# Final SSD states with the state dimension as stationary operand, in rounded products, three of four groups behind the mixer norm's sums

## The chip, the cores and the metric

The kernel runs on one core of a Trainium2 chip. The metric is the device time of one execution in microseconds (us). The engines that matter here are TensorE (PE, matrix products; its weight loads are listed as PEld), VectorE (DVE), ScalarE (ACT), GpSimd (POOL, which also issues DMAs) and SyncE (SP, which issues most of the DMAs).

## The reference

One layer of a streaming encoder, for a prompt of 256 new frames and for a sample of 32 next frames of a running stream, with the same weights. All of it is computed in full precision:

```python
proj = rmsnorm(x) @ w_in                       # u_pool | z | x, B, C | dt
y_pool = pool_mixer(u_pool)                    # trailing means, windows 2, 4, 8, 16
y_ssd, new_ssd = ssd_mixer(z, xBC, dt, state)  # Mamba-2 scan, gated, normed
mix = concat([y_pool, y_ssd]) @ w_out          # 3072 -> 2048
x = x + rmsnorm(mix, norm_mix_post)
up = conv3(rmsnorm(x, norm_ffn_pre) @ w_up)    # 2048 -> 11264
x = x + rmsnorm((silu(gate) * val) @ w_down, norm_ffn_post)   # 5632 -> 2048
```

The change is about one output of the mixer, the final state of the scan. For each of 32 heads (64 channels each; 16 heads share one B of 128 values)

```python
state[head, channel, n] = decay * state_before[head, channel, n] \
    + sum over tokens of  w[token, head] * x[token, head, channel] * B[token, n]
```

where `w` is the time step times the decay from the token to the end. The prompt starts with a state of zero; the sample has a state before. So the prompt's state is a product over 256 tokens and the sample's one over 32 tokens plus a scaled history, each 2048 channels by 128 values. Outputs are `y` for both streams, these states, and the last rows of the convolutions and the pooling.

## The kernel before, in words

**Products.** Activations stand transposed, channels on the 128 partitions and the 288 tokens (256 of the prompt, then 32 of the sample) in the columns. Each full-precision product of the projections is made of three products of rounded operands (`fp32r`): the activation is split into a rounded part and the rest, the weight into `whi` and `wlo`, and `mm3` (L141 to L144) adds high by high, high by low and low by high in one accumulator. A weight tile comes by a DMA that SP issues (`fetch_w`, L117, 1 MB into `raw`), ACT rounds it (`whi`, L136) and DVE subtracts (`wlo`, L137). `project` runs over the K pieces of a projection and, for each piece, over the column groups (256 columns, two accumulators each). `raw`, `whi` and `wlo` have a few buffers each, so that loads run some tiles ahead.

**Order.** The instructions of each engine are put in order by a planner that simulates the queues; `tc.high_priority` moves an instruction ahead of its place in the program, `pin` and `tc.keep_in_program_order` hold it to it. Tiles of one `tag` share its `bufs` buffers; who asks for a tile waits until an older one of the tag is done with.

**The w_out stage.** Its activations are `mixp` (eight pooling tiles) and `mixs` (sixteen SSD tiles). Seven calls of `project` cover column groups (0, 1), 2, 3, 4, 5, 6, 7; the K pieces of each are tiles 8 to 15, 16 to 23 and 0 to 7. When an accumulator is done, `mix_out` squares it on ACT, POOL adds the square to `msum` (`sq_add`, L677), and ACT writes the scaled copy `mg` to SBUF. The sum over the 2048 channels, which are spread over partitions, is a product with a matrix of ones in full precision: `msum` of the first fourteen tiles goes in at the start of group 7 (L956), and the squares of the last two follow by themselves (L852). Then come the root (L976, ACT), the reciprocal (L977, DVE), for each of sixteen tiles a multiplication and the addition of the residual (L988, L989, DVE), and the rounded and the low part of `hn` (L993 on ACT, L994 on DVE), which the w_up products read. `xsum` (L1002, L1006) collects squares for the next norm.

**The states.** Earlier, the scan has written the convolved x and B by token to DRAM (`xs_d`, `b_d`), and the weights `w` to `tokd`. The states are products in full precision (not split; the profile counts two PE instructions for each):

- `states_of(g)`, g = 0, 1, each four tiles of 128 channels, after w_out groups 2 and 4. POOL issues seven loads (x of the prompt, x of the sample, state before), DVE multiplies by `w` and the decay, and PE makes, for each tile, two products over 128 prompt tokens (L905) and one over the 32 sample tokens on 32 partitions (L911). The stationary operand is x by token, the moving one B: channels come out on partitions, n in 128 columns. ACT copies, DVE adds the history, SP stores.
- `state_in(t)` and `state_mm(t)`, t = 8 to 15, one tile of 128 channels each: three loads on POOL (L926), two multiplications on DVE, three products (L938; for the sample the last 128 tokens, with B set to zero where they are the prompt's). `state_mm(8)` stands between the last two sums of the norm, the other seven behind them, ahead of the first `hn` product on PE. ACT copies (L942), POOL adds the history (L943), SP stores two tiles (L944, L945).
- `pwq` is a set of four small products that spread the sample's `w` over four sets of 32 partitions, at the start of the w_out stage.

The buffers `du` (four, of the size of two 288-column tiles) hold pooling tiles at the start of the stage and the operands of the states after it.

## Time and profile before

| | |
|---|---|
| median of three runs | 1336.0 us (1335.72 to 1336.15) |
| span of the profiled execution (first to last instruction) | 1333.3 us |
| time around that span, by the median | 2.7 us |
| PE busy | 1325.7 us, 99% |
| DVE, ACT, POOL busy | 885.5 us (66%), 665.1 us (50%), 241.7 us (18%) |
| w_out stage | about 303 to 475 us |
| norm, from the last w_out product to the first `hn` product | 475.1 to 481.5 us |
| w_up (with w_down in turns from 762 us), then the end of w_down | 481.5 to 1324.9 us |
| granted PE clock | 1.000 |

The page gives the profiled execution its span alone, without a time of its own beside it. In the rows of the timeline the columns are the start in us, the length in us, the engine, the line of the kernel, the operation and the tiles it writes and reads, with "xN" for N instructions drawn together; in brackets stands how long the engine had been idle before, and what ended that. In the rows of groups, the numbers behind the bar are the busy time in us, the mean of one in ns, and, after the second bar, the idle time before them. PE's instructions overlap in its pipeline: the time that one takes from the stream is the distance of starts, not the length of a row. A row with two or more products runs from the first start to the last end.

### The profile page before, as it was taken

What the parts mean: (1) busy time and instruction counts of PE and PEld (TensorE: products, weight loads), DVE (VectorE), ACT (ScalarE), POOL (GpSimd) and SP (SyncE); (2) the same over time, 40 slices, a digit from 0 to 9 for tenths busy, and PEclk for the clock granted to TensorE, in tenths of its full rate; (3) what the DMA queues carried; (4) which work ended last, traced back from release to release, by engine and by line L of the source; (5) the groups of instructions that cost most, each with busy time, mean ns of one, the idle gap of its engine ahead of it and who ended that gap; (6) DMA issues with size and microseconds to landing.
All of it is one profiled execution on the core that took longest, in us unless ns stands there. A gap on an engine that the chain in (4) does not pass through costs nothing.

```text
span 1333.3 us, 25388 instructions
## 1 busy us (share of the span) xinstructions
PE 1325.7 (99%) x10127; PEld 1314.2 (99%) x10127; DVE 885.5 (66%) x1501; ACT 665.1 (50%) x995; POOL 241.7 (18%) x386
## 2 busy tenths in 40 slices
PE   9999999999999999999999999999999999999998
PEld 9999999999999999999999999999999999999997
DVE  7999987879544488976766643335666666754454
ACT  7557767446443456544444433334454444444442
POOL 2343231222122310211211200001121111201110
PEclk9999999999999999999999999999999999999999
DMA  8678884455555446766554454454554555466753
GB/s 329 192 216 266 272 252 156 155 199 210 190 191 202 143 145 227 210 184 181 167 177 158 153 172 156 160 182 162 179 165 159 167 170 170 159 227 188 206 177 111
DMA packets 110230, 249.52 MB, mean 187 GB/s; under 512 B 64480, under 2 KB 75840, under 8 KB 87584
## 3 DMA queue, kind: packets, MB, share of 16 engines
q1 hardware_dynamic: 105920, 233.61, 54.6%
q0 software_dynamic: 3808, 13.77, 2.9%
q8 instruction: 79, 1.29, 0.4%
q10 hardware_dynamic: 384, 0.52, 0.1%
q14 instruction: 39, 0.32, 0.1%
HBM read 235.91 MB, written 11.95 MB: 186 GB/s over the span
## 4 chain that ended last, share of the span: by engine, by line
PE 98%; DVE 0%; DMA 0%; ACT 0%; SPq 0%; issue 0%
PE acc L142 30%; PE acc L144 30%; PE acc L143 30%; PE acc L355 2%; PE acc_x L355 1%; PE py L613 1%; PE acc L1200 0%; PE acc L1201 0%; DMA xg<-in_x_g 0%; PE acc_t L1223 0%; PE pst L938 0%; PE acc_x L143 0%; PE acc_x L142 0%; PE acc_x L144 0%; PE pst L905 0%; PE py L615 0%
## 5 line engine op out<-in xcount | busy, mean ns | idle before, releaser
L137 DVE TENSOR_TENSOR wlo<-raw,whi 128x1024 fp32r<-128x1024 f32 (+1 forms) x396 | 472.0, 1193 | 346.1 <-ACT whi L136 344.8
L136 ACT ACTIVATE whi<-raw 128x1024 fp32r<-128x1024 f32 (+1 forms) x396 | 408.5, 1033 | 503.2 <-PE acc L143 420.4
L142 PE MATMUL acc<-hn,whi 128*128 128x288 f32 x1376 | 404.3, 296 | 0.0
L143 PE MATMUL acc<-hn,whi 128*128 128x288 f32 x1376 | 403.8, 294 | 0.2 <-DVE hn L994 0.2
L144 PE MATMUL acc<-hn,wlo 128*128 128x288 f32 x1376 | 403.3, 294 | 0.0
L143 PEld LDWEIGHTS acc<-hn,whi 128*128 128x128 f32 x1376 | 259.9, 189 | 0.7 <-DVE hn L994 0.7
L144 PEld LDWEIGHTS acc<-hn,wlo 128*128 128x128 f32 x1376 | 259.9, 189 | 0.0
L142 PEld LDWEIGHTS acc<-hn,whi 128*128 128x128 f32 x1376 | 257.3, 187 | 0.1
L142 PE MATMUL acc<-fa,whi 128*128 128x288 f32 x660 | 195.5, 296 | 0.0
L143 PE MATMUL acc<-fa,whi 128*128 128x288 f32 x660 | 195.4, 296 | 0.0
L144 PE MATMUL acc<-fa,wlo 128*128 128x288 f32 x660 | 195.1, 296 | 0.0
L142 PE MATMUL acc<-xn,whi 128*128 128x288 f32 x608 | 180.8, 297 | 0.0
L143 PE MATMUL acc<-xn,whi 128*128 128x288 f32 x608 | 179.1, 295 | 0.0
L144 PE MATMUL acc<-xn,wlo 128*128 128x288 f32 x608 | 178.8, 294 | 0.0
L143 PEld LDWEIGHTS acc<-fa,whi 128*128 128x128 f32 x660 | 124.5, 189 | 0.0
L142 PEld LDWEIGHTS acc<-fa,whi 128*128 128x128 f32 x660 | 124.1, 188 | 0.0
L144 PEld LDWEIGHTS acc<-fa,wlo 128*128 128x128 f32 x660 | 123.8, 188 | 0.0
L1027 POOL COPY fc_stage<-ebuf 128x4 f32<-128x4 f32 x88 | 25.7, 293 | 503.5 <-DVE ebuf L1026 460.1
L143 PEld LDWEIGHTS acc<-xn,whi 128*128 128x128 f32 x608 | 114.9, 189 | 0.1
L144 PEld LDWEIGHTS acc<-xn,wlo 128*128 128x128 f32 x608 | 114.8, 189 | 0.0
L142 PEld LDWEIGHTS acc<-xn,whi 128*128 128x128 f32 x608 | 114.0, 187 | 0.8 <-issue 0.5
L1033 DVE SCALAR_TENSOR_TENSOR fc<-ebuf,cols,fc 128x290 f32<-128x290 f32 x176 | 90.4, 517 | 2.9 <-ACT fc L1031 0.3
(333 smaller groups left out, 1766.5 us busy)
## 6 DMA issues: line engine op xcount, KB each, us to landing
raw<-in_w_up SPq DMA_DIRECT2D x80, 1024.0 KB, 5.1
raw<-in_w_in SPq DMA_DIRECT2D x38, 1024.0 KB, 5.4
raw<-in_w_down SPq DMA_DIRECT2D x32, 1024.0 KB, 5.0
raw<-in_w_out SPq DMA_DIRECT2D x24, 1024.0 KB, 5.0
raw<-in_w_down SPq DMA_DIRECT2D x16, 768.0 KB, 4.2
raw<-in_w_up SPq DMA_DIRECT2D x14, 512.0 KB, 3.9
gb<-g_d POOLq DMA_DIRECT2D x8, 832.0 KB, 7.1
raw<-in_w_first SPq DMA_DIRECT2D x5, 768.0 KB, 13.0
```

What stands on the lines that cost most here:

```text
L136: act.activation(hi, raw[:, k : k + n, :], AF.Copy)
L137: dve.tensor_tensor(lo, raw[:, k : k + n, :], hi.bitcast(F32), op=ALU.subtract)
L142: then(pe.matmul(out, wh, a[:, 0, :], start=start, stop=False))
L143: then(pe.matmul(out, wh, a[:, 1, :], start=False, stop=False))
L144: then(pe.matmul(out, wl, a[:, 0, :], start=False, stop=stop))
L355: pin(pe.matmul(first[m], w[:, k, r * NB + m * P :][:, :P], xn[kb + k][:, x, :], start=kb + k + r + x == 0, stop=kb + k == KD - 1 and r == ...
L613: ins = pe.matmul(y[c, 0:256], xw[:, 0, f_], m[:, h, 0:256], start=True, stop=False)
L1027: pool.tensor_copy(fc_stage[:, :, :, i], e[:, 256:324].rearrange("p (s c) -> p s c", c=34)[:, :, 0:2])
L1033: dve.scalar_tensor_tensor(c, e[:, r_ : r_ + 290], f_w[:, r_, i : i + 1], c, op0=ALU.mult, op1=ALU.add)
```

## The change

- **The other way round.** The stationary operand of a state product is now B by token (128 tokens by 128 values of n) and the moving one x times `w` with 512 channels: n comes out on partitions and 512 channels in the columns. Four groups g = 0 to 3 of 512 channels take the place of two `states_of` and eight `state_mm`. The state outputs are laid out (n, channel), and the host turns them.
- **Rounded products.** B is split once into `bt_h` and `bt_l`, x times `w` for each group into `xh` (ACT) and `xl` (DVE), and a prompt's group takes six products (two blocks of 128 tokens, each high by high, high by low, low by high).
- **96 partitions.** The sample's 32 tokens stand three times above each other, x as (high, low, high) and B as (high, high, low), so that one product over 96 partitions sums the three terms. `raw_s` and `xq` are loaded three times for it, and `pwq` makes `w` for 96 partitions; it moves to an earlier place, beside `phv`, which gets a second small product for the decays.
- **History.** `history` loads 256 channels of the state before at a time (POOL), multiplies by the decay (DVE) and writes the result to a DRAM tile `hd` (SP), after w_out groups 2 to 5. `state_out` copies a group's two accumulators (ACT), stores the prompt's (SP), adds `hd` to the sample's by a DMA that accumulates (POOL's queue), and stores that (SP).
- **Place.** Group 0 is made after w_out group 2. The operands of group 1 are prepared after group 4, those of groups 2 and 3 after group 5. The products of group 1 come behind the last w_out product, five of them ahead of the norm's sums and two behind; groups 2 and 3 follow behind the sums, and the copies of group 3 stand behind the second tile's `hn`.
- **The norm's sums.** Column groups 6 and 7 go through `project` together. The early sum at group 7 leaves. `msum` takes fifteen squares, the last square stays by itself, both are split into a rounded and a low part, and four rounded products with a rounded matrix of ones follow. `xsum` uses the buffer of `msum`.
- **Buffers.** `du` has six instead of four and takes the pooling tiles' `dpool` as well. The first group's outputs `ho` and the raw operands `xr` are in it; groups 2 and 3 keep their split operands in the buffers of the `hn` tiles (`atile`).

The diff, cut to its core (the removed functions are named above):

```diff
+    p_ = aux([P, HEADS], "pwq")
+    wq = const.tile([P, HEADS], F32, name="wq")
+    for j in range(3):
+        pe.matmul(p_[NS * j : NS * (j + 1), :], ident[:, P - NS :], tokd[:, 2, :], start=True, stop=True)
+    dve.tensor_copy(wq[: 3 * NS], p_[: 3 * NS])
+    hv = htile("hv", NX + HEADS)
     elast = htile("elast", 1)
     act.activation(elast, g[:, 415:416], AF.Exp)
     dve.tensor_scalar(hv[:, 0:NX], pick, hp[:, 2:3], None, op0=ALU.mult)
-    dve.tensor_scalar(hv[:, NX:], pick, elast, None, op0=ALU.mult)
-    p_ = aux([P, 2 * NX], "phv")
-    pe.matmul(p_, sel64.rearrange("h r q -> h (r q)"), hv, start=True, stop=True)
-    dcol = const.tile([P, 2 * NX], F32, name="dcol")
+    dve.tensor_scalar(hv[:, NX:], id32, elast, None, op0=ALU.mult)
+    p_ = aux([P, NX + HEADS], "phv")
+    pe.matmul(p_[:, :NX], sel64.rearrange("h r q -> h (r q)"), hv[:, :NX], start=True, stop=True)
+    pe.matmul(p_[:, NX:], ones[:HEADS, :], hv[:, NX:], start=True, stop=True)
+    dcol = const.tile([P, NX + HEADS], F32, name="dcol")
...
-        d = op_.tile([P, NT], F32, tag="dpool", bufs=2, name="dpool")
+        d = op_.tile([P, 2, NT], F32R, tag="du", bufs=6, name="dpool")[:, 0, :].bitcast(F32)
...
-        a = op_.tile([P, 2, NT], F32R, tag="du", bufs=4, name="du")
+        a = op_.tile([P, 2, NT], F32R, tag="du", bufs=6, name="du")
...
+    ones_r = op_.tile([P, P], F32R, name="ones_r")
+    act.activation(ones_r, ones, AF.Copy)
...
-    last_sq = []
     def mix_out(p_):
         m = len(x1)
         o = btile("mg")
         if m < KD - 2:
             sq_add(msum, p_, op_, m == 0)
+        elif m == KD - 2:
+            with tc.high_priority(offset=400):
+                q = op_.tile([P, NT], F32, tag="sq", bufs=2, name="sq")
+                act.activation(q, p_, AF.Square)
+                dve.tensor_tensor(msum, msum, q, op=ALU.add)
         else:
-            q = op_.tile([P, NT], F32, name=f"msq{m}")
             with tc.high_priority(offset=400):
-                act.activation(q, p_, AF.Square)
-            last_sq.append(q)
-        if m == KD - 1:
-            for i, q in enumerate(last_sq):
-                if i:
-                    state_mm(LATE, *late_in[0])
-                tc.keep_in_program_order(pe.matmul(p_m, ones, q, start=False, stop=i == 1))
+                lows_ = op_.tile([P, 2, NT], F32R, tag="du", bufs=6, name="mlo")
+                last_sq = op_.tile([P, 318], F32, tag="win", bufs=3, name="last_sq")[:, :NT]
+                parts = [lows_[:, 0, :], lows_[:, 1, :]]
+                for i, q in enumerate((msum, last_sq)):
+                    h_ = op_.tile([P, NT], F32R, tag="sq", bufs=2, name="mhi")
+                    if i:
+                        pin(act.activation(q, p_, AF.Square))
+                        pin(dve.tensor_copy(h_, q))
+                    else:
+                        pin(act.activation(h_, q, AF.Copy))
+                    pin(dve.tensor_tensor(parts[i], q, h_.bitcast(F32), op=ALU.subtract))
+                    parts.append(h_)
+            def sums():
+                for i, q in enumerate((2, 0, 3, 1)):
+                    pin(pe.matmul(p_m, ones_r, parts[q], start=i == 0, stop=i == 3))
+            state_mm(1, *state_ops[1], between=sums)
...
-    btok = op_.tile([P, 2, 3, P], F32, name="btok")
...
+    bt_h, bt_l = (op_.tile([P, 2, 2, P], F32R, name=n) for n in ("bt_h", "bt_l"))
+    bt_s = bpool.tile([P, NT], F32R, tag="b", name="bt_s")[:, : 2 * P].rearrange("p (g c) -> p g c", g=2)
+    raw_b = op_.tile([P, 2, NT], F32, tag="du", bufs=6, name="raw_b")
+    raw_b = raw_b.rearrange("p r c -> p (r c)")[:, : 4 * P].rearrange("p (g b c) -> p g b c", g=2, b=2)
+    raw_s = op_.tile([P, 318], F32, tag="win", bufs=3, name="raw_s")[: 3 * NS, : 2 * P]
     for gi in range(2):
         c = slice(gi * P, (gi + 1) * P)
-        sp.dma_start(out=btok[:, gi, 0:2, :], in_=b_d[:NP_, c].rearrange("(b p) c -> p b c", p=P))
-        if gi:
-            pool.memset(btok[: P - NS, gi, 2, :], 0.0)
-            sp.dma_start(out=btok[P - NS :, gi, 2, :], in_=b_d[NP_:, c])
+        sp.dma_start(out=raw_b[:, gi], in_=b_d[:NP_, c].rearrange("(b p) c -> p b c", p=P))
+    for j in range(3):
+        sp.dma_start(out=raw_s[NS * j : NS * (j + 1), :], in_=b_d[NP_:, :])
+    act.activation(bt_h, raw_b, AF.Copy)
+    dve.tensor_tensor(bt_l, raw_b, bt_h.bitcast(F32), op=ALU.subtract)
+    s_ = bt_s.rearrange("p g c -> p (g c)")
...
+    act.activation(s_[: 3 * NS], raw_s, AF.Copy)
+    rows_ = slice(2 * NS, 3 * NS)
+    dve.tensor_tensor(s_[rows_], raw_s[rows_], s_[rows_].bitcast(F32), op=ALU.subtract)
...
+    def unit(name, ahead_=False):
+        t = atile(name) if ahead_ else op_.tile([P, 2, NT], F32R, tag="du", bufs=6, name=name)
+        return t.rearrange("p r c -> p (r c)")[:, : 4 * P]
+    def state_in(g, ahead_=False):
+        xl = [unit("xl", ahead_) for _ in range(2)]
+        xh = [unit("xh", ahead_) for _ in range(2)]
+        s = unit("xs", ahead_)
+        for b in range(2):
+            raw = unit("xr").bitcast(F32)
+            for i in range(2):
+                pool.dma_start(
+                    out=raw[:, 2 * P * i : 2 * P * (i + 1)], in_=xs_d[2 * g + i][b * P : (b + 1) * P, :]
+                )
+            o = raw.rearrange("p (r q) -> p r q", r=8)
+            w = tokd[:, b, 8 * g : 8 * g + 8]
+            dve.tensor_tensor(o, o, w.unsqueeze(2).broadcast_to([P, 8, 64]), op=ALU.mult)
+            act.activation(xh[b], raw, AF.Copy)
+            dve.tensor_tensor(xl[b], raw, xh[b].bitcast(F32), op=ALU.subtract)
+        for i in range(2):
+            c = slice(2 * P * i, 2 * P * (i + 1))
+            t = op_.tile([P, 318], F32, tag="win", bufs=3, name="xq")[: 3 * NS, : 2 * P]
+            for j in range(3):
+                pool.dma_start(out=t[NS * j : NS * (j + 1), :], in_=xs_d[2 * g + i][NP_:, :])
+            o = t.rearrange("p (r q) -> p r q", r=4)
+            heads = slice(8 * g + 4 * i, 8 * g + 4 * i + 4)
+            dve.tensor_tensor(o, o, wq[: 3 * NS, heads].unsqueeze(2).broadcast_to([3 * NS, 4, 64]), op=ALU.mult)
+            act.activation(s[: 3 * NS, c], t, AF.Copy)
+            r_ = slice(NS, 2 * NS)
+            dve.tensor_tensor(s[r_, c], t[r_], s[r_, c].bitcast(F32), op=ALU.subtract)
+        return xh, xl, s
+    hd = dram.tile([P, D_SSD], F32, name="hd")
+    def history(g):
+        for i in range(2):
+            heads = slice(8 * g + 4 * i, 8 * g + 4 * i + 4)
+            c = slice(4 * P * g + 2 * P * i, 4 * P * g + 2 * P * (i + 1))
+            h = btile("h")[:, : 2 * P]
+            pool.dma_start(out=h, in_=state_nq[:, c])
+            o = h.rearrange("p (r q) -> p r q", r=4)
+            w = dcol[:, NX:][:, heads]
+            dve.tensor_tensor(o, o, w.unsqueeze(2).broadcast_to([P, 4, 64]), op=ALU.mult)
+            sp.dma_start(out=hd[:, c], in_=h)
...
+    def state_mm(g, xh, xl, s, between=None):
+        gi = g // 2
+        st = acc_ps.tile([P, 4 * P], F32, tag="acc", name="pst")
+        st_s = aux([P, 4 * P], "pst") if g < 3 else acc_ps.tile([P, 4 * P], F32, tag="acc", name="pst")
+        todo = [(bt_h, xh, 0), (bt_h, xl, 0), (bt_l, xh, 0), (bt_h, xh, 1), (bt_h, xl, 1), (bt_l, xh, 1)]
+        for i, (w_, x_, b) in enumerate(todo):
+            if between and i == 5:
+                between()
+            pin(pe.matmul(st, w_[:, gi, b, :], x_[b], start=i == 0, stop=i == 5))
+        pin(pe.matmul(st_s, bt_s[: 3 * NS, gi, :], s[: 3 * NS], start=True, stop=True))
+        if g == 3:
+            return [g, st, st_s]
+        state_out(g, st, st_s)
+    def state_out(g, st, st_s):
+        if g:
+            ho, ho_s = (op_.tile([P, 2 * NT], F32, tag=f"mixp{2 * g - 2 + i}", bufs=1, name="ho") for i in range(2))
         else:
+            ho, ho_s = (unit("ho").bitcast(F32) for _ in range(2))
+        ho, ho_s = ho[:, : 4 * P], ho_s[:, : 4 * P]
+        for o, s in ((ho, st), (ho_s, st_s)):
+            ins = act.activation(o, s, AF.Copy)
+            if g == 3:
+                pin(ins)
+        c = slice(4 * P * g, 4 * P * (g + 1))
+        sp.dma_start(out=new_ssd_p[:, c], in_=ho)
+        pool.dma_start(out=ho_s, in_=hd[:, c], accum_op=ALU.add)
+        sp.dma_start(out=new_ssd_s[:, c], in_=ho_s)
+    state_ops = {}
...
-            if g == 7 and kb == 0:
-                pe.matmul(p_m, ones, msum, start=True, stop=False)
...
-    for grp in ((0, 1), (2,), (3,), (4,), (5,), (6,), (7,)):
+    for grp in ((0, 1), (2,), (3,), (4,), (5,), (6, 7)):
...
-        if grp[0] in (2, 4):
-            states_of(grp[0] // 2 - 1)
-        elif grp[0] == 6:
-            late_in[:] = [state_in(t, t >= LATE + 4) for t in range(LATE, NX - 2)]
+        if 2 <= grp[0] < 6:
+            history(grp[0] - 2)
+        if grp[0] == 2:
+            state_mm(0, *state_in(0))
+        elif grp[0] == 4:
+            state_ops[1] = state_in(1)
+        elif grp[0] == 5:
+            state_ops[2] = state_in(2, True)
+            state_ops[3] = state_in(3, True)
...
-    late_in += [state_in(t, ahead_=True) for t in range(NX - 2, NX)]
...
-    for t in range(LATE + 1, NX):
-        state_mm(t, *late_in[t - LATE])
+    for g in (2, 3):
+        still = state_mm(g, *state_ops[g])
...
-    xsum = op_.tile([P, NT], F32, name="xsum")
+    xsum = msum
...
+            if t == 1:
+                state_out(*still)
...
-    (1, 1, 32, 64, 128), (1, 1, 32, 64, 128), (P, 2 * 2 * 2 * NF),
+    (P, D_SSD), (P, D_SSD), (P, 2 * 2 * 2 * NF),
...
-        "state_ssd": v["state_ssd"],
...
-    return (y_p, y_s, *rows(pools, 15), *rows(sconvs, 3), ssd_p, ssd_s, *rows(fconvs, 2))
+    states = [a.T.reshape(1, 1, HEADS, -1, P) for a in (ssd_p, ssd_s)]
+    return (y_p, y_s, *rows(pools, 15), *rows(sconvs, 3), *states, *rows(fconvs, 2))
```

More of the change, by code (lines that the diff above doesn't have):

```diff
@@ L65, in body @@
     heads_in,
-    state_ssd,
     state_nq,
@@ L522, in body @@
         dve.tensor_copy(tokd[:, b, :], p_[:, 2, :])
-    hv = htile("hv", 2 * NX)
+    p_ = aux([P, HEADS], "pwq")
[4 more added lines that the diff above has]
+    hv = htile("hv", NX + HEADS)
     elast = htile("elast", 1)
@@ L788, in pool_parts @@
     def pool_parts(i):
-        a = op_.tile([P, 2, NT], F32R, tag="du", bufs=4, name="du")
+        a = op_.tile([P, 2, NT], F32R, tag="du", bufs=6, name="du")
         for o, n, c in ((0, NP_, 15), (NP_, NS, 286)):
@@ L934, in state_mm @@
-    def state_mm(t, xp, xq, h):
-        gi = t // 8
-        st = acc_ps.tile([P, 2, P], F32, tag="acc", name="pst")
-        for o, x_, b in ((0, xp[:, :P], 0), (0, xp[:, P:], 1), (1, xq, 2)):
-            pin(pe.matmul(st[:, o, :], x_, btok[:, gi, b, :], start=b != 1, stop=b != 0))
-        ho = op_.tile([P, 2 * NT], F32, tag=f"mixp{t - LATE}", bufs=1, name="ho")
-        ho = ho[:, : 2 * P].rearrange("p (r c) -> p r c", r=2)
-        act.activation(ho, st, AF.Copy)
-        pool.tensor_tensor(ho[:, 1, :], ho[:, 1, :], h, op=ALU.add)
-        sp.dma_start(out=hpv[:, t, :], in_=ho[:, 0, :])
-        sp.dma_start(out=hsv[:, t, :], in_=ho[:, 1, :])
```

66 lines of the change are left out of this document (removed).

## The prediction

> **What bounds the kernel now.** I read the page first, then the chain of waits, then the timeline of the places where the states are made, because a kernel that keeps one engine busy for the whole span can gain only what leaves that engine's stream.
>
> ```profile
> span 1333.3 us, 25388 instructions
> PE 1325.7 (99%) x10127; PEld 1314.2 (99%) x10127; DVE 885.5 (66%) x1501; ACT 665.1 (50%) x995; POOL 241.7 (18%) x386
> ...
> PE 98%; DVE 0%; DMA 0%; ACT 0%; SPq 0%; issue 0%
> ```
>
> The reader is to see that TensorE (PE) is the chain: 98% of the span follows it. One product with 288 columns costs 0.13 us of its stream (pitch of the rows below), although a single one lasts 0.29. So each product taken out gives its pitch, and each new idle gap of PE takes the gap back. Times are worked out against this profiled execution. The page gives its span alone, 1333.3 us; the median of the runs is 1336.0, so 2.7 us lie around the span, and I carry differences of the span over to the median.
>
> **What leaves PE's stream.** The two early groups are made by `states_of` after the projections of `w_out` groups 2 and 4. The first of them stands in the timeline so, and the second (415.0 us) has the same length:
>
> ```profile
> 374.37 0.29 PE L144 MATMUL acc<-mixp,wlo 128*128 128x288 f32 x1
> 374.50 1.95 PE L905 MATMUL pst<-btok,xw 128*128 128x128 f32 x16
> 376.38 0.50 PE L911 MATMUL pst<-btok,xq 32*128 32x128 f32 x8
> 376.81 0.40 PE L142 MATMUL acc<-mixs,whi 128*128 128x288 f32 x1
> 377.05 0.29 PE L143 MATMUL acc<-mixs,whi 128*128 128x288 f32 x1
> ...
> 461.88 0.65 PE L956 MATMUL psum_m<-msum,ones 128*128 128x288 f32 x2
> 462.15 0.51 PE L142 MATMUL acc<-mixs,whi 128*128 128x288 f32 x1
> 462.49 0.29 PE L143 MATMUL acc<-mixs,whi 128*128 128x288 f32 x1
> ```
>
> A full-precision product counts two instructions here, of 0.11 us each at 128 columns. From 374.50 to 376.81 are 2.31 us, and the next ordinary product comes after 0.24 instead of 0.13: 2.42 us per group, 4.84 for both. The early sum of squares (L956) takes 0.27 and then 0.34 instead of 0.13: 0.48. Both leave, 5.32 us.
>
> What comes in their place is `state_mm(0)`, seven rounded products with 512 columns. No row has 512; the widest are these:
>
> ```profile
> 1318.23 0.31 PE L1200 MATMUL acc<-fa,wlast 128*128 128x320 f32 x1
> 1318.38 0.29 PE L1201 MATMUL acc<-fa,wlast 128*128 128x288 f32 x1
> 1318.80 2.93 PE L1223 MATMUL acc_t<-whi,fa 128*128 128x256 f32 x24
> ```
>
> 256 columns have a pitch of (2.93-0.28)/23 = 0.115, 320 of 0.15; by this slope 512 would have 0.235 (estimate), and seven take 1.65 us. Bounds: 0.20 (two of 256 less their overhead) and 0.26 (by the slope from 288 to 320), 1.4 to 1.8. [...]
>
> The four small `pwq` products move to the earlier product `phv`, which gets a second small one: taken as nothing, between -0.4 (all hidden in a switch of form that is there anyway) and +0.2. **Before the norm PE thus saves 5.32-1.65 = 3.67 us.**
>
> **The norm's sums.** This is where the change adds a wait. Now:
>
> ```profile
> 473.07 1.23 DVE L137 TENSOR_TENSOR wlo<-raw,whi 128x1024 fp32r<-128x1024 f32 x1 [1.28 <-ACT whi L136]
> 473.69 0.41 ACT L846 ACTIVATE msq<-acc 128x288 f32<-128x288 f32 x1 [0.66 <-PE acc L144]
> 475.08 0.65 PE L852 MATMUL psum_m<-msq,ones 128*128 128x288 f32 x2
> 475.15 0.63 ACT L136 ACTIVATE whi<-raw 128x512 fp32r<-128x512 f32 x1 [0.65 <-PE acc L143]
> 475.57 0.83 PE L938 MATMUL pst<-btok,xw 128*128 128x128 f32 x6
> 475.69 0.39 ACT L846 ACTIVATE msq<-acc 128x288 f32<-128x288 f32 x1
> 475.81 0.69 DVE L137 TENSOR_TENSOR wlo<-raw,whi 128x512 fp32r<-128x512 f32 x1 [1.52 <-ACT whi L136]
> 476.23 0.65 PE L852 MATMUL psum_m<-msq,ones 128*128 128x288 f32 x2
> 476.92 0.50 ACT L976 ACTIVATE rm<-psum_m,eps_t 128x288 f32<-128x288 f32 x1
> 477.46 1.95 DVE L977 RECIPROCAL rm<-rm 128x288 f32<-128x288 f32 x1 [0.95 <-ACT rm L976]
> 478.72 0.46 POOL L943 TENSOR_TENSOR ho<-ho,xw 128x128 f32<-128x128 f32 x1 [0.21 <-ACT ho L942]
> 478.73 2.84 PE L938 MATMUL pst<-btok,xw_a 128*128 128x128 f32 x24
> 479.44 0.72 DVE L988 TENSOR_TENSOR mg<-mg,rm 128x288 f32<-128x288 f32 x1
> 480.20 0.64 DVE L989 TENSOR_TENSOR mg<-mg,xT 128x288 f32<-128x288 f32 x1
> 480.87 0.54 ACT L993 ACTIVATE hn<-mg,cols 128x288 fp32r<-128x288 f32 x1 [0.21 <-DVE mg L989]
> 481.46 0.67 PE L142 MATMUL acc<-hn,whi 128*128 128x288 f32 x3
> ...
> L1006 DVE TENSOR_TENSOR xsum<-xsum,sq 128x288 f32<-128x288 f32 x15 | 6.8, 453 | 0.1
> ```
>
> PE fills 475.08 to 481.46 (6.38 us) with two sums and eight state tiles and does not wait, while the other chain (last sum, square root, reciprocal, two DVE steps, `hn`) ends at the same moment. There is no slack on either side. Afterwards PE has here 21 products of 512 (4.94) and four sums of 0.13: 5.46, so the chain will decide. It gets longer: behind the last square (now to 476.08, and I add 0.1 for `mhi` of `msum`, a pass like L846 that stands ahead of the 512-wide `whi` on ACT and partly in its idle time) the order on DVE has that weight's `wlo` (to 476.6), then the copy `mhi`, then the subtraction (0.45), and only then the last sum may start. A copy of this form is shown by two rows, far apart:
>
> ```profile
> 3.86 1.67 DVE L305 CAST w<-raw 128x256 fp32r<-128x256 f32 x1 [2.62 <-DMA raw<-in_w_first]
> ...
> 4.01 1.36 POOL L333 MEMSET ubuf<- 128x350 f32 x4
> ...
> L550 DVE COPY cbt<-pcb 128x128 f32<-128x128 f32 x2 | 0.6, 280 | 0.0
> ```
>
> The first has the form, but it ended at 5.53, 0.16 after POOL's memsets (5.37), as if it had waited for them; POOL has no arithmetic at the norm now. I take 0.3 and keep 1.67 for a rival. [...]
>
> So the last sum starts at 476.6+0.3+0.5 = 477.45, is read at 477.75; root 0.5, reciprocal 1.95, then two DVE steps at 0.45 each instead of 0.72 and 0.64, because POOL's eight adds (L943) leave, and `hn` 0.54, with gaps of 0.03: PE starts on `hn` at 481.87 instead of 481.46. **Loss 0.41**, with 0.86 if the DVE steps stay slow. PE is idle some 1.3 us in this stretch. Behind it PE begins with five accumulators instead of six, because the other two are held by the last group until ACT has copied it. Two places follow. The low part of the first `hn` (DVE, 0.51 behind two steps for the next tile) is now covered by five products instead of six (0.13 less), while those two steps are shorter by 0.3: nothing. And the two copies stand on ACT behind two `hn` and two squares; at 0.63 each (the 512-wide `whi` above) they end some 2.6 us after PE's start, while PE has 20 products (2.6 us) and the wait for the low part ahead of the accumulators they free: nothing, or 0.3 at the worst.
>
> **What else moves.** ACT and DVE get the rounding and the subtraction of 512-wide tiles (0.63 and 0.69 each, by the rows above), POOL issues 52 DMAs for the states instead of 38, and SP 21 instead of 27, among them eight writes of scaled history, each of which waits for POOL's load and DVE's multiplication with weight loads queued behind it. What hides it:
>
> ```profile
> L136 ACT ACTIVATE whi<-raw 128x1024 fp32r<-128x1024 f32 x41 | 43.5, 1061 | 73.9 <-PE acc L143 71.7 <-DVE xw L931 2.1
> ...
> SPq L121 <- DVE wlo L137: 122.0, 22, 7.6
> ...
> 492.42 5.16 SPq L121 DMA_DIRECT2D raw<-in_w_up  x4
> ```
>
> In 345 to 475 us ACT waits for PE to free weight tiles (71.7 us) and SP for DVE to free loads (122.0 us in 22 waits, the longest 7.6). A tile is ready 1.06+1.23 us after its buffer is free and is used three tiles later; one tile is 24 products, 24x0.132 = 3.17 us, so 9.5-2.3, some 7 us of delay, cost nothing. If that cover is gone, PE waits for each further microsecond. At the norm eight `w_up` loads stand ahead of the state stores on SP, as now, and the next four behind them are issued at 492.42, when DVE has freed their tiles. The last store waits for POOL's accumulating DMA, an operation that no row of before shows; the nearest are POOL's state loads, which land 2.5 to 5.5 us after their issue (row below). Its source is copied by 484.6 (2.6 us after PE's start, above), issue 0.7, so SP is free by 487.8 to 490.8, ahead of 492.4: nothing, and each microsecond beyond costs one behind it.
>
> **Sum.** 3.67 saved, 0.41 lost: 3.26 us, 1336.0 - 3.2 = 1332.8.
>
> **The rivals.** *The norm's chain gets longer still.* If the copy lasts 1.67, the sum is 1.4 less: 1334.2. For it: the only row of this form. Against: POOL's memsets beside it.
>
> *Slower: one buffer for eight loads.* Group 1 holds five of the six `du` buffers until the norm, so the raw tiles of groups 2 and 3 go through the sixth one after another, in three rounds: DMA, multiply, round, subtract, and DVE takes them in order between its `wlo`.
>
> ```profile
> L926 POOL DMA_DIRECT2D xw<-xs_d x4: 710/710/712, 418.0 to 426.6; - x4
> ...
> DMA to landing us min/median/max: 2.5/3.1/5.5
> ...
> L894 DVE TENSOR_TENSOR xw<-xw,tokd 128x512 f32<-128x512 f32 x4 | 2.7, 688 | 1.3 <-DMA xw<-xs_d 1.3
> ```
>
> A round is 0.6 (first issue) + landing + 0.69 + 1.23 (a `wlo` between) + 0.7: 6.3 us at the median landing of 3.1, just the two weight tiles (6.34) that PE works on meanwhile. The rounds begin about 3 us early, so the norm is late by three times the landing over 3.1, less 3: it decides from 4.1 on, and at 5.5 it is 4.2 us late, 1337.0. Against: the median is well under 4.1, and state loads beside weight loads have mostly landed in it.
>
> *The change does not do what it says.* If a rounded product with 512 columns took half as much again, 0.35, `state_mm(0)` would cost 0.8 more, and the 16 products behind the sums 5.6 us instead of 3.76, past the chain by 1.3: about 1335, within the noise of no change. Against: the pitch grows by 0.5 ns per column in every row.
>
> **How the numbers follow.** 0.2% (2.7 us) is about what a measurement of this kernel can tell from no change. Forecast 0.5 (1332.0 to 1333.8 by its own bounds: weights of 1.4 to 1.8, steps of 0.45 or 0.7, `pwq`); longer chain 0.22; one buffer 0.2; wide products 0.08. The forecast at 1332.8 is 0.24% faster, so a part of its chance (0.08) falls within 0.2%, as do the longer chain and the wide products; of the one buffer 0.02 stays within and 0.18 is slower. Faster 0.42, same 0.40, slower 0.18. The range leaves out less than one in ten on each side: 1331.7 to 1336.8.
>
> **What would show it.** Right: seven `pst` products of a pitch near 0.235 at about 374; no `psum_m` row near 460; PE idle before the third and fourth sum and before the first `hn` product, 1.3 us together; the copy `mhi` at 0.3; the DVE steps of the norm (L988 of before) at 0.45. Wrong: the copy over 1 us, DVE waiting for the `xr` DMA with `wlo` running late into the norm, PE idle in front of a `whi`, or a store on SP ahead of a late weight load.

## The result, and the profile after

The changed kernel takes 1331.9 us (median of 8 runs, 1331.0 to 1332.9) against 1335.7 us for the kernel before beside it (1334.8 to 1336.2). The ratio is 0.9971, with a 95% interval of 0.9963 to 0.9979: 3.8 us or 0.29% faster, where 1332.8 had been forecast. A second set of runs of the same kernel (below) gave 1331.9 and 0.9972. In each of these runs the time is 1.7 or 1.8 us longer than the span of the same execution; so about 1 us of the 2.7 that the table ahead of the prediction gives as time around the span is something else, a profiled execution of the kernel before that was shorter than the median (estimate, from the 1.7).

The page of the changed kernel, the lines that answer to those shown of before:

```profile
span 1330.1 us, 25269 instructions
PE 1321.7 (99%) x10057; PEld 1309.2 (98%) x10057; DVE 894.9 (67%) x1512; ACT 672.3 (51%) x1007; POOL 242.4 (18%) x391
...
PE 98%; DVE 1%; DMA 0%; ACT 0%; SPq 0%; issue 0%
```

PE is still the chain. Its busy time fell by 4.0 us, and 1% of the chain has become DVE: the chain of waits below shows that it now leaves PE in the norm, where PE's work filled the stretch before.

Group 0, the first state group, in the timeline (start, length, engine, line, operation and tiles):

```profile
375.12 0.29 PE L143 MATMUL acc<-mixp,wlo 128*128 128x288 f32 x1
375.25 0.39 PE L950 MATMUL pst<-xh,bt_h 128*128 128x512 f32 x1
...
376.64 0.40 PE L951 MATMUL pst<-xs,bt_s 96*128 96x512 f32 x1
376.87 0.30 PE L141 MATMUL acc<-mixs,whi 128*128 128x288 f32 x1
```

Seven products take 376.87 - 375.25 = 1.62 us, 0.231 each; the one on 96 partitions starts 0.24 after its predecessor and is followed after 0.23, so neither it nor the return to ordinary products costs a switch. Rows of the norm, picked from the same view:

```profile
471.90 0.29 PE L143 MATMUL acc<-mixp,wlo 128*128 128x288 f32 x1
472.63 0.39 ACT L860 ACTIVATE last_sq<-acc 128x288 f32<-128x288 f32 x1
473.37 0.30 DVE L861 CAST mhi<-last_sq 128x288 fp32r<-128x288 f32 x1
473.73 0.40 PE L869 MATMUL psum_m<-mhi,ones_r 128*128 128x288 f32 x1
477.18 0.46 DVE L1014 TENSOR_TENSOR mg<-mg,rm 128x288 f32<-128x288 f32 x1
478.75 0.67 PE L141 MATMUL acc<-hn,whi 128*128 128x288 f32 x3 [0.39 <-ACT hn L1019]
```

From the start of the last w_out product to that of the first `hn` product it is 478.75 - 471.90 = 6.85 us. Before it was 6.51, from the row here to the first `hn` product at 481.46:

```profile
474.95 0.29 PE L144 MATMUL acc<-mixp,wlo 128*128 128x288 f32 x1
```

The chain of waits through the norm of the changed kernel (start, length, what; the pieces called issue, 0.02 to 0.04 us each, are left out):

```profile
471.93 0.14 PE acc L142
472.09 0.64 ACT whi L135
472.76 0.69 DVE wlo L136
473.45 0.23 DVE mhi L861
473.71 0.47 DVE mlo L864
474.22 0.41 PE psum_m L869
474.66 0.51 ACT rm L1002
475.19 1.96 DVE rm L1003
477.18 0.47 DVE mg L1014
477.67 0.47 DVE mg L1015
478.16 0.54 ACT hn L1019
478.75 0.67 PE acc L141 x3
```

The last square is not on it. It is there at 473.02, but the cast has to wait on DVE for the `wlo` of a w_up weight, which waits for that weight's rounding on ACT.

Where the time went, from the starts of the same PE instructions in both traces (us):

| stretch | before | after | difference |
|---|---|---|---|
| start of the span to product 100 of the first projection | 20.00 | 20.62 | +0.62 |
| to the first `mixs` product of w_out | 293.94 | 294.14 | +0.20 |
| to the first state product | 60.56 | 60.49 | -0.07 |
| to the last w_out product | 100.45 | 96.65 | -3.80 |
| to the first `hn` product (the norm) | 6.51 | 6.85 | +0.34 |
| to the end | 851.80 | 851.33 | -0.47 |

The first row is the same work in both kernels; the experiments show that it changes from execution to execution (product 100 started between 19.6 and 21.3 us in the twelve traces here). Without it the sum is -3.80, as large as the difference of the medians.

### The profile page after: what moved, and what is told of

It is laid out like the page before. It is cut to its first block, busy times and chain, and to the rows that moved or that the text cites. A ratio compares the mean times of both kernels' runs of the same rounds, so it can differ in the third digit from the quotient of the medians.

```text
span 1330.1 us, 25269 instructions
## 1 busy us (share of the span) xinstructions
PE 1321.7 (99%) x10057; PEld 1309.2 (98%) x10057; DVE 894.9 (67%) x1512; ACT 672.3 (51%) x1007; POOL 242.4 (18%) x391
## 4 chain that ended last, share of the span: by engine, by line
PE 98%; DVE 1%; DMA 0%; ACT 0%; SPq 0%; issue 0%
PE acc L141 30%; PE acc L143 30%; PE acc L142 30%; PE acc L354 2%; PE acc_x L354 1%; PE py L616 1%; PE acc L1228 0%; DMA xg<-in_x_g 0%; PE acc L1229 0%; PE acc_t L1251 0%; PE acc_x L142 0%; PE acc_x L141 0%; PE acc_x L143 0%; PE py L618 0%; DVE wlo L136 0%
```

## The experiments

Each kernel was run beside the kernel before on the same chip, ratios are against it. An interval is some 0.1% wide to each side (1.2 us), so smaller effects are read from the places of PE instructions in the trace. With `pwq` back, group 1 early, one product and three products the time is 1.8 to 2.1 us longer than the span instead of 1.7, so 0.1 to 0.4 us of their times are not in the stretches of the trace. All diffs are against the changed kernel. "The norm" is the distance from the last w_out product to the first `hn` product, 6.85 us in the changed kernel.

**The changed kernel again, and the place of `pwq`.** One run has no edit, the other moves the small products back:

```diff
-    p_ = aux([P, HEADS], "pwq")
...
-    dve.tensor_copy(wq[: 3 * NS], p_[: 3 * NS])
     hv = htile("hv", NX + HEADS)
...
     dve.tensor_tensor(s_[rows_], raw_s[rows_], s_[rows_].bitcast(F32), op=ALU.subtract)
+    p_ = aux([P, HEADS], "pwq")
...
+    dve.tensor_copy(wq[: 3 * NS], p_[: 3 * NS])
```

> The changed kernel once more, unchanged. The profiled execution of the changed kernel reached product 100 of the first projection at 20.6 us, that of the kernel before at 20.0, other variants at 19.7 to 21.3, though their first 100 products are the same. Theory, the start varies from execution to execution and the rest does not: the start lies anywhere in 19.7 to 21.3, and from there to the end it takes 1309.5 us within 0.1; time 1331.5 to 1332.3. Rival, the start is a property of the kernel: 20.6 again.

> The changed kernel with the small products that spread the sample's weights (pwq) back at the start of the w_out stage. Theory, the move costs next to nothing: from product 100 of the first projection to the first mixs product PE takes 294.14 us in the changed kernel and 293.94 before; with pwq back it takes 293.9 to 294.1, the stretch from there to the first state product takes 0.3 us longer, as it did before (60.56 against 60.49 with other work in it), and the time is the same within 0.4 us. Rival, the move is a part of the gain: 0.4 us or more slower.

Again: 1331.9 us, 0.9972 (0.9961 to 0.9984). Its execution reached product 100 at 19.92 us, 0.7 earlier than the first, and from there it took 1309.50 us against 1309.46. So the start varied and the rest did not, and the +0.62 of the table is no part of the change. With `pwq` back: 1332.2 us, 0.9976 (0.9966 to 0.9986); from product 100 to the first `mixs` product 294.19 (changed 294.14, before 293.94), to the first state product 60.54 (60.49). Neither stretch moved as the theory had it (293.9 to 294.1, and 0.3 longer); the time stayed within its 0.4. The place of `pwq` is worth 0.1 us, as good as nothing; the 0.2 us that the change adds in the first stretch stay when `pwq` goes back, so they belong to what else differs there (the second product of `phv` and an order that came out differently), which was not separated.

**Group 1 taken out of the norm.**

```diff
-            state_mm(1, *state_ops[1], between=sums)
+            sums()
...
-            state_ops[1] = state_in(1)
+            state_mm(1, *state_in(1))
```

> The changed kernel, but group 1's seven products stand behind w_out group 4, where its operands are made, and not around the norm's sums. Theory, the place gives the gain: the seven products cost 1.6 us in the w_out stream (7 x 0.231) and nothing comes back at the norm, where PE idles that much longer; time 1.6 us above the changed kernel. Rival, the rounding alone gives the gain and the place nothing: the norm gets shorter by what the w_out stage gets longer, no difference.

1333.6 us, 0.9985 (0.9976 to 0.9993), 1.7 us above the changed kernel. The stretch from the first state product to the last w_out product is 1.7 us longer, of which the seven products are 1.6, and the norm is not a bit shorter (6.86):

```profile
479.56 0.66 PE L141 MATMUL acc<-hn,whi 128*128 128x288 f32 x3 [0.88 <-ACT hn L1019]
```

PE waits 0.88 instead of 0.39 us in front of `hn`, and 0.63 between the second and the third sum. The place behind the last w_out product is worth the whole cost of a group.

**Fewer products behind the sums.** One prompt product in place of six for groups 1 to 3, and then three (the prompt's states of these groups are left incomplete):

```diff
-        for i, (w_, x_, b) in enumerate(todo):
-            if between and i == 5:
+        last = 2 if g else 5
+        for i, (w_, x_, b) in enumerate(todo[: last + 1]):
+            if between and i == 2:
                 between()
-            pin(pe.matmul(st, w_[:, gi, b, :], x_[b], start=i == 0, stop=i == 5))
+            pin(pe.matmul(st, w_[:, gi, b, :], x_[b], start=i == 0, stop=i == last))
```

(The first has `last = 0 if g else 5` and the sums ahead of the products.)

> The changed kernel, but groups 1, 2 and 3 make one prompt product each instead of six (the prompt's states of these groups are left incomplete), so 15 products of 0.231 us, 3.5 us of PE work, leave the stretch between the last w_out product and the first hn product. Theory, the chain of sum, root, reciprocal and DVE steps decides: the first hn product stays where it is, within 0.2 us, PE idles 3.5 us more, and the time is the same. Rival, PE's work decides that stretch: up to 3.5 us faster.

> The changed kernel with three prompt products for each of groups 1, 2 and 3 instead of six (their prompt states are left incomplete); nine products less, 2.1 us of PE work. With one product each, PE idled 2.7 us before the first hn product and then ran at half pace for 3.4 us, which made that kernel 1.2 us slower than the changed one. Theory, the slow clock follows a long enough idle stretch: here PE idles about 1.6 us before the first hn product; if that is too short for it, the products behind keep 0.13 us and the time is that of the changed kernel; if not, they take 0.24 us for some 3 us and the time is 1 to 1.5 us longer. Either way the first hn product stays where it is within 0.2 us. Rival, the half pace of that run came from something else: no relation to the idle stretch.

With one product 1333.0 us, 0.9982 (0.9973 to 0.9991); with three 1332.1 us, 0.9974 (0.9964 to 0.9984). The norm stays at 6.85 us in both, though 3.5 and 2.1 us of PE work have left it: the chain of sum, root, reciprocal and DVE steps decides its length, and the products behind the sums are free. But the time did not stay the same in both: with one product it is 1.1 us longer than that of the changed kernel, with three 0.2. Timelines and stretches of the kernel with one product, then of that with three (in a row of stretches: length, busy time of PE, PEld, DVE, ACT and POOL with instructions, then the granted PE clock):

```profile
478.96 0.66 PE L141 MATMUL acc<-hn,whi 128*128 128x288 f32 x3 [2.71 <-ACT hn L1020]
480.75 0.44 PE L143 MATMUL acc<-hn,wlo 128*128 128x288 f32 x1
480.99 0.44 PE L142 MATMUL acc_x<-hn,whi 128*128 128x288 f32 x1
...
480.00:482.00 2.00, 2.00 (x11) 2.00 (x10) 1.93 (x5) 2.00 (x6) 0.63 (x1) 0.52 0.91 147
482.00:484.00 2.00, 2.00 (x12) 2.00 (x12) 1.97 (x6) 1.32 (x3) 0.24 (x1) 0.62 0.80 134
```

```profile
478.85 0.74 PE L141 MATMUL acc<-hn,whi 128*128 128x288 f32 x3 [1.77 <-ACT hn L1020]
...
478.00:480.00 2.00, 1.15 (x6) 1.15 (x7) 1.93 (x6) 1.74 (x5) 0.38 (x1) 0.82 0.90 161
480.00:482.00 2.00, 2.00 (x10) 2.00 (x9) 1.97 (x5) 2.00 (x5) 0.74 (x1) 0.50 0.91 148
482.00:484.00 2.00, 2.00 (x14) 2.00 (x14) 1.97 (x6) 1.23 (x3) 0.12 (x1) 0.83 0.71 142
```

In these two executions, after PE had idled for 2.71 and 1.77 us, the granted clock fell to 0.50, and products of 288 columns followed each other after 0.24 us instead of 0.13. From the means of the stretches (a mean of 0.52 over 2 us is 1.92 us at half) it lasted 1.92 + 1.52 = 3.4 us in the first and 0.72 + 2.00 + 0.68 = 3.4 in the second. That cost 1.5 us behind the first `hn` product in each; 0.7 of it came back in the next 40 us, where the changed kernel's PE itself waited a little for weights. So the state products have a second use here: they keep PE at its pace while the norm runs.

Not every execution seems to have paid this. A stretch of 3.4 us at half lowers the mean clock of a run of 1331 us by 0.0013 (estimate, from the 3.4). With one product, the two executions of eleven with a mean clock of 0.999 took 1331.7 and 1331.8 us, as long as the changed kernel, and the nine with 0.997 or 0.998 took 1332.7 to 1334.6. With three products, five of eight have 0.999 and took 1331.7 to 1332.2; the one in the trace is among the three others, 1332.3 to 1333.1. No trace of an execution without the fall was kept, so this is read from the runs' figures alone.

**The sums in full precision.**

```diff
-                lows_ = op_.tile([P, 2, NT], F32R, tag="du", bufs=6, name="mlo")
...
+                pin(act.activation(last_sq, p_, AF.Square))
...
-                for i, q in enumerate((2, 0, 3, 1)):
-                    pin(pe.matmul(p_m, ones_r, parts[q], start=i == 0, stop=i == 3))
+                for i, q in enumerate((msum, last_sq)):
+                    pin(pe.matmul(p_m, ones, q, start=i == 0, stop=i == 1))
```

> The changed kernel, but the norm's sum is made of two full-precision products (msum, then the last square) in place of four rounded ones, so the cast, the two subtractions and the rounding of msum leave. Theory, the chain from the last square to the first hn product decides the norm's length: the last sum starts at once behind the last square instead of 1.2 us later, and takes 0.3 us longer; the first hn product comes 0.6 to 0.9 us earlier behind the last w_out product (6.0 to 6.3 us instead of 6.85), PE's wait of 0.39 us before it goes, and the time falls by about 0.6 us against the changed kernel. Rival, PE's own work decides: two full-precision sums cost 0.5 us more than four rounded ones, and the time grows by that.

1331.2 us, 0.9970 (0.9959 to 0.9981): 0.7 us under the changed kernel, which is within the intervals. The norm is 6.55 us, 0.30 shorter, half of what was expected: the sum of the last square no longer waits for the cast and the subtraction, but it stands behind five state products and the first sum.

```profile
472.86 0.65 PE L857 MATMUL psum_m<-last_sq,ones 128*128 128x288 f32 x2
...
477.64 0.67 PE L141 MATMUL acc<-hn,whi 128*128 128x288 f32 x3 [0.41 <-ACT hn L1007]
```

The square was there at 472.22 (ACT, 471.83 + 0.39), 0.64 us before its sum began. So the sums, still in full precision, were moved forward:

```diff
-            if between and i == 5:
-                between()
+            if between and i in (2, 4):
+                between(i // 2 - 1)
...
+            def sums(i):
+                pin(pe.matmul(p_m, ones, (msum, last_sq)[i], start=i == 0, stop=i == 1))
```

> Full-precision norm sums in the changed kernel, placed earlier between group 1's products: msum behind the second, the last square behind the fourth, instead of both behind the fifth. With both behind the fifth the first hn product stood 6.55 us behind the last w_out product's start. Theory, the chain decides: the last sum starts when the last square is there, 0.4 to 0.6 us earlier, and the first hn product stands 5.95 to 6.15 us behind; PE's own work (21 products of 0.233, two sums of 0.48) sets a floor of 5.98; time 0.7 to 0.9 us under the changed kernel. Rival, PE already decides there: no gain over the sums behind the fifth product.

1331.0 us, 0.9965 (0.9952 to 0.9978), the shortest of all kernels here, if not beyond the interval against the changed kernel. The norm is 6.32 us, not 5.95 to 6.15: the last sum starts 0.41 us behind the square instead of 0.64, and PE's wait ahead of `hn` is down to 0.17. What is left is PE's own work, 6.02 us, the 0.13 of the last w_out product and this wait. Both rivals hold a part: the chain decided until here, and now PE's own work is within 0.17 us of it. A further way to shorten the chain, the cast ahead of the weight's `wlo` on DVE, was not tried.

**POOL at work during the norm.**

```diff
+        if m == KD - 1:
+            spare = op_.tile([P, 2 * NT], F32, tag="mixp7", bufs=1, name="spare")[:, :NT]
+            for _ in range(6):
+                pool.tensor_tensor(spare, x1[12], x1[13], op=ALU.add)
```

> The changed kernel, with six additions of 128x288 on POOL added behind the last w_out product, whose result nobody reads, so that POOL computes while the norm runs. Theory, POOL's additions slowed the norm's DVE steps before the change and their absence is a part of why the norm's chain lengthened by only 0.34 us: the cast of the last square takes more than 0.30 us (up to the rest of a POOL addition, 0.8 to 1.5 us), the subtraction, the multiplication and the addition about 0.7 instead of 0.46, the first hn product comes 0.6 to 2 us later, and the time grows by 0.6 to 2 us. Rival, POOL's work does not touch DVE's: same durations and same time.

1334.5 us, 0.9991 (0.9982 to 1.0000), 2.6 us above the changed kernel, more than the 0.6 to 2 expected; the norm is 9.26 us. In the timeline:

```profile
472.81 4.90 POOL L876 TENSOR_TENSOR spare<-mg 128x288 f32<-128x288 f32 x5 [3.53 <-PE acc L143]
473.23 1.10 DVE L136 TENSOR_TENSOR wlo<-raw,whi 128x512 fp32r<-128x512 f32 x1
474.25 0.89 DVE L861 CAST mhi<-last_sq 128x288 fp32r<-128x288 f32 x1
475.18 0.98 DVE L864 TENSOR_TENSOR mlo<-last_sq,mhi 128x288 fp32r<-128x288 f32 x1
...
477.19 1.95 DVE L1007 RECIPROCAL rm<-rm 128x288 f32<-128x288 f32 x1 [1.03 <-ACT rm L1006]
...
479.04 1.14 POOL L876 TENSOR_TENSOR spare<-mg 128x288 f32<-128x288 f32 x1
479.18 1.33 DVE L1018 TENSOR_TENSOR mg<-mg,rm 128x288 f32<-128x288 f32 x1
```

The casts, subtractions and multiplications of DVE that begin beside a POOL addition are longer: the weight's `wlo` 1.10 instead of 0.69, the cast 0.89 instead of 0.30, the subtraction 0.98 and the multiplication 1.33 instead of 0.46. The reciprocal, which ran beside the end of the fifth addition (to 477.71), kept its 1.95. The lengthened steps add 0.41 + 0.59 + 0.52 + 0.87 = 2.4 us, which is what the norm grew by. The multiplication ended 0.33 us after the 1.14 us addition it met; whether DVE waits for POOL's instruction there or runs slower beside it was not separated.

**Column groups 6 and 7 apart.**

```diff
-    for grp in ((0, 1), (2,), (3,), (4,), (5,), (6, 7)):
+    for grp in ((0, 1), (2,), (3,), (4,), (5,), (6,), (7,)):
```

> The changed kernel, but w_out column groups 6 and 7 go one after the other, as before the change. Theory: the order in which they are made moves nothing on the path, the last accumulator ends at the same time and the time is the same within 0.3 us. Rival, drawing the two groups together is part of the gain (an earlier end of the fifteen squares): 0.5 to 1 us slower, with the sums later behind the last w_out product.

1336.6 us, 1.0009 (1.0000 to 1.0017): 4.8 us above the changed kernel. Both expectations missed. The executions lie far apart, 1335.3 to 1338.4, and the one in the trace is the longest of the eleven: 6.6 us above that of the changed kernel. Nearly all of that is the norm, which takes 13.13 us, 6.3 more. The steps of the last raw tiles, in the changed kernel and then with the groups apart:

```profile
442.53 0.63 ACT L912 ACTIVATE xh<-xr 128x512 fp32r<-128x512 f32 x1 [1.06 <-PE acc L143]
...
457.32 1.11 POOL L906 DMA_DIRECT2D xr<-xs_d  x2 [4.26 <-DVE xl L913]
...
462.98 0.68 DVE L913 TENSOR_TENSOR xl<-xr,xh 128x512 fp32r<-128x512 f32 x1
```

```profile
455.56 0.63 ACT L912 ACTIVATE xh<-xr 128x512 fp32r<-128x512 f32 x1 [0.37 <-PE acc L143]
...
470.04 1.11 POOL L906 DMA_DIRECT2D xr<-xs_d  x2 [3.72 <-DVE xl L913]
...
476.09 0.69 DVE L911 TENSOR_TENSOR xr<-xr,tokd 128x512 f32<-128x512 f32 x1 [3.71 <-DMA xr<-xs_d]
476.70 0.45 DVE L864 TENSOR_TENSOR mlo<-msum,mhi 128x288 fp32r<-128x288 f32 x1
477.21 0.40 PE L869 MATMUL psum_m<-mlo,ones_r 128*128 128x288 f32 x1 [3.37 <-DVE mlo L864]
...
477.89 0.69 DVE L913 TENSOR_TENSOR xl<-xr,xh 128x512 fp32r<-128x512 f32 x1
```

The first rounding of group 2 (`xh`) takes the buffer of the first `mixs` tile and waits for PE's last product with that tile. With groups 6 and 7 drawn together that product belongs to the first K piece of both, at 442.5 us; with the groups apart it comes at the start of group 7, at 455.6. Three rounds through the one free `du` buffer follow in either case: 6.3 to 6.8 us each in the changed kernel; 6.5, 6.3 and 8.8 with the groups apart, where the loads of the last round took up to 5.4 us to land instead of the median 3.2. They end at 463.7 in the one, 8.5 us ahead of the norm's first subtraction (`mlo`, 472.19), and at 478.6, in the middle of the norm, in the other.

It is not the buffer that holds `mlo`: the late tile is still to be read by its own subtraction at 477.89 when `mlo` begins at 476.70. It is DVE's order. The multiplication of the late tile (L911) stands ahead of `mlo` there and waits 3.71 us for its load, and `mlo` follows it at once. PE waits 3.37 us for `mlo`, and then also runs at half pace, so that its state products hold the first `hn` product up for another 0.8 us (485.39, where `hn` is there at 484.57).

To see whether the wait of `mlo` is all, the same with full-precision sums, which need no `mlo`:

```diff
-    for grp in ((0, 1), (2,), (3,), (4,), (5,), (6, 7)):
+    for grp in ((0, 1), (2,), (3,), (4,), (5,), (6,), (7,)):
...
-                lows_ = op_.tile([P, 2, NT], F32R, tag="du", bufs=6, name="mlo")
...
+                for i, q in enumerate((msum, last_sq)):
+                    pin(pe.matmul(p_m, ones, q, start=i == 0, stop=i == 1))
```

> Column groups 6 and 7 apart as in the slow run with them apart, and full-precision norm sums, which need no split buffer. Theory, that run lost its time because the last mixs read of the first K piece came 13 us later, so that the split operands of groups 2 and 3, which take mixs buffers, and behind them the raw tiles in the one free du buffer came late, and the low part of msum had to wait for this buffer (3.4 us), after which PE ran at half pace: without the low part the sums are in time, PE waits at most 1.5 us in front of group 3's products, and the time is 1332 to 1333. Rival, the order of the groups itself costs the time, or the operands of group 3 are as late as the low part was: 1335 or more.

1335.8 us, 1.0001 (0.9992 to 1.0009), so the rival's number; the norm is 9.52 us. The wait for `mlo` is gone, but another has taken its place:

```profile
475.67 0.69 DVE L899 TENSOR_TENSOR xr<-xr,tokd 128x512 f32<-128x512 f32 x1 [2.93 <-DMA xr<-xs_d]
477.55 0.48 ACT L990 ACTIVATE rm<-psum_m,eps_t 128x288 f32<-128x288 f32 x1
...
482.13 1.09 PE L141 MATMUL acc<-hn,whi 128*128 128x288 f32 x3 [3.04 <-ACT hn L1007]
```

The norm's sums are done by 475.1, but ACT has the late tile's roundings ahead of the root in its order, and starts the root at 477.55. The cause is the late tile; which of the norm's steps it holds depends on what stands behind it on ACT and DVE. A larger `du`, which would do away with the rounds, was not tried.

## Why the prediction was right, point by point

- **What leaves PE's stream: right.** 3.67 us were worked out ahead of the norm. From product 100 to the last w_out product the traces have 454.95 and 451.28 us: 3.67. That the last digit agrees is luck: the stretch with the state products gave 3.80, and the first stretch, which the prediction had at nothing, took 0.20 back. The wide products have 0.231 instead of 0.235 us each, the product on 96 partitions starts 0.24 behind its predecessor and is followed after 0.23, no dearer than the others, and the place of `pwq` is worth 0.1 (around its products the trace of before has 0.66 us from 313.52 to 314.18, where two pitches of 0.13 would be 0.26). The 0.235 does not come out of the slope that is named for it: 0.115 at 256 columns and 0.5 ns for each column more give 0.243, the row of 320 columns 0.255 (estimates); the figure taken was the nearer one. The rival of 0.35 us a product falls. What the other way round and the rounding gave in group 0 (2.42 - 1.62 = 0.80 us) and the 0.48 of the early sum are read from rows; no run took them back one by one.
- **The norm's chain decides: right, and shown.** 0.41 us longer was forecast, 0.34 measured. PE stands idle for 1.35 us of the norm, as forecast (1.3): 21 products of 0.231 and five of 0.13 fill 5.5 of the 6.85. The cast took the 0.30 taken for it; the DVE steps take 0.46 now that POOL's additions are gone, against 0.72 and 0.64 in the rows of before, and one of them took 1.33 when POOL was put to work again; and 15 products less change nothing in the length of the norm.
- **A longer chain (the copy at 1.67): fell here,** but its reason stands: with POOL at work the same cast takes 0.89.
- **One buffer for the raw tiles: the mechanism was right, its place in time was not.** The step "the rounds begin about 3 us early" is wrong: they end 8.5 us ahead of the norm's first subtraction, at a median landing of 3.2 and rounds of 6.3 to 6.8. What sets their start is the last use of a `mixs` tile, and that depends on drawing groups 6 and 7 together, an edit that the prediction did not cost at all. Without it this rival is what happens, down to the sign that the prediction gave for it (DVE waiting for the `xr` load in the norm), and the gain is gone.
- **Behind the norm: "nothing" was 0.47 us too little.** The wait for the low part of the first `hn` (0.2 before) is gone, since the DVE steps ahead of it are shorter; 0.1 more goes in a wait for weights at about 517 us and 0.16 near the end, which was not followed up.
- **Sum.** -3.26 was forecast, -3.80 measured without the start of the span: 0.07 of the difference from the norm, 0.47 from behind it. The forecast of 1332.8 also started from a median of 1336.0 in three runs, where the eight runs beside the changed kernel have 1335.7.

## What to carry to other kernels

When PE is the bound, put work that nothing waits for behind the last input of a norm: up to the length of the norm's chain it is free (taking 3.5 us of it out left the norm at 6.85 us here), and it spares PE the slow pace that followed idle stretches here (0.24 instead of 0.13 us a product for 3.4 us, after waits of 1.77 us and more). When an edit only changes the order of loops, follow every buffer whose last use moves, to whoever waits for it and to what stands behind that instruction on its engine; here 13 us of such a move decided 4.8 us. And keep POOL's arithmetic out of a stretch in which DVE is the chain: six additions of POOL made the norm 2.4 us longer here.

## What the runs showed of the hardware that was not expected

PE's pace after an idle stretch. After waits of 1.77, 2.71, 3.04 and 3.37 us in the norm (three products a group, one, groups apart with full sums, groups apart) the granted clock was 0.50, for 3.4 us in the first three and for 6.8, twice that, in the last. Products of 288 columns then came every 0.24 us, and in the last, where the slow stretch lies ahead of the first `hn` product, state products of 512 columns every 0.43. After waits of 0.88 (group 1 early) and 1.27 us (POOL busy) the clock stayed at 1.00.

The clock does not fall at the end of a wait. The stretches of 1 us in which it fell, with three products, with one, with the groups apart and full sums, and with the groups apart (columns as above, the granted clock is the third figure from the end):

```profile
479.00:480.00 1.00, 1.00 (x6) 1.00 (x7) 0.97 (x4) 1.00 (x4) 0.00 (x0) 0.64 1.08 160
```

```profile
480.00:481.00 1.00, 1.00 (x7) 1.00 (x6) 0.96 (x3) 1.00 (x4) 0.00 (x0) 0.55 0.77 119
```

```profile
481.00:482.00 1.00, 0.00 (x0) 0.00 (x0) 0.93 (x4) 0.46 (x2) 0.13 (x1) 0.87 0.61 82
```

```profile
477.00:478.00 1.00, 0.40 (x1) 0.19 (x1) 1.00 (x4) 1.00 (x3) 0.00 (x0) 0.78 0.00 0
```

A mean of 0.64 over 1 us is 0.72 us at half, so with three products the clock fell at 479.28, and worked out in the same way at 480.10 with one: 0.4 and 1.1 us behind the first `hn` product. With the groups apart and full sums it fell at 481.74, 0.4 us ahead of that product, while PE was still waiting; with the groups apart at 477.56, 0.35 us behind the end of the wait for `mlo`. What sets the moment was not shown. Nor was it shown why the clock seems to have fallen in some executions of the same kernel and not in others.
